# Hybrid decoder layer: the first half of x turned by plain products with the identity, the first weights loaded ahead of x's second tile, and linear attention's outputs by chunks in quarters of the array

## The chip, the cores and the metric

One core of a Trainium2 chip. The metric is device microseconds of one execution, median over runs; less is better. Before the change three runs gave 434.2, 435.39 and 435.99 us, median 435.39.

## What is computed

One decoder layer on 256 tokens of width 1024, in fp32. Cut to what the change touches:

```python
n    = rmsnorm(h, attn_norm)
proj = n @ w_in            # columns: g_q|g_k (512), g_v (512), g_r, g_al, d_q, d_k, d_v, gate_a, gate_b
# gated linear attention, chunks of 64 tokens, 4 heads, DK 64, DV 128
att     = einsum('bhncd,bhnsd->bhncs', q_dec, k_inv);  att = where(causal, att, 0)
o_intra = einsum('bhncs,bhnsv->bhncv', att, vc)
o_inter = einsum('bhncd,bhndv->bhncv', q_dec, s_prev)
o = o_intra + o_inter
...                        # differential attention, branch products, w_out, residual
h = h + hierarchical_moe(rmsnorm(h))     # 32 experts, top 2
h = h + sigmoid(h @ w_ple_gate) * rmsnorm(p @ w_ple);  out = rmsnorm(h, final_norm)
```

## The kernel before, in words

Tokens are two tiles `t` of 128. The first stage (to about 194 us) is a list of 114 *units*, most of them as follows: a unit is one 128x512 piece of a weight matrix (256 KB). `raw_load` (L342) issues its load on SP's queue; `part` (L350) splits it into a high half (ScalarE copy, tile `..._h`) and a low half (VectorE subtract, tile `..._l`), because every product is done as three fp32r products (`mm3`, L416: high x high, high times low of x, low times high of x). The unit then runs six products of 512 columns, three for each token tile. `run` (L388) is the loop that orders everything by hand: it loads eight units ahead, splits three units ahead (`part(i + a)` for `a < 3`, then `part(i + 3)` after the unit's products), and every engine keeps program order (`Ordered`, L50, and L58, the one line under which all instructions stand).

x comes as four quarters of 128x512: token tile `t`, column half `n` (`load_x`, L121). TensorE turns it: `x_transposed(q)` (L298) makes eight transposes into two PSUM banks `pxT0q`, `pxT1q`; `x_parts(k)` (L304) copies block `k` of the turned x out of the banks into `xT` as a high half (ScalarE, with the gain `g_attn`) and a low half (VectorE). The first eight units (`gqk_0` to `gqk_7`, L454) are the eight blocks of x against the columns for g_q and g_k; `part(i)` for `i < 8` also makes `x_parts(i)`. Before the first unit TensorE runs two dummy products (`warm`, L138) on a tile of ones that VectorE fills (L136), and one small transpose `pv` (L294) for `g_attn`.

Linear attention (`gla_steps`, L541) runs between units. Its last part (L593 to 613), for each `t`: the bank `po` takes, for four heads, the masked scores `attT` (128x128, off-diagonal 64x64 blocks zero) times the values, and then for each 64-token chunk `c` two products of the decayed queries with the state. fp32 operands (not fp32r) go through TensorE as two passes: two records in the trace for one product.

After the first stage come the router and the experts: eight groups of four experts, whose weights are loaded into a ring of slots (`refill`, L217), a slot being free when the products on it are done.

Of the kernel before, what the change touches and what calls it, by code (L numbers as in the profile page):

```python
# [20 lines left out]
P = 128  # L21
T = 256
NT = T // P
D = 1024
KC = D // P
# [38 lines left out]
def kernel(  # L64
# [33 lines left out]
    def bank(name):  # L98
        return psb.tile([P, 512], F32, tag="pb", name=name)

    V, A, E, Y, Q = (Ordered(tc, e) for e in (nc.vector, nc.scalar, nc.tensor, nc.sync, nc.gpsimd))
# [6 lines left out]
    xn = slot(NSLOT - 1, [NT, D], F32, "xn")  # L108
    tmp = slot(9, [2048], F32, "tmp")
    early = slot(6, [2048], F32, "early")  # L110
# [10 lines left out]
    def load_x(t, n):  # L121
        Y.dma_start(xn[:, t, n * 512:(n + 1) * 512], xs[t * P:(t + 1) * P, n * 512:(n + 1) * 512])

    load_x(0, 0)
    Y.dma_start(av, attn_norm[0].rearrange("(k p) -> k p", p=P))
    load_x(1, 0)
    Q.dma_start(posi, positions[0].rearrange("(t p) -> t p", p=P))
    wr = cst.tile([P, KC, 40], F32, name="wr")
    brt = cst.tile([P, 40], F32, name="brt")


    warm = cst.tile([P, 1], F32, name="warm")
    V.memset(warm, 0.0)
    A.activation(warm, warm, AF.Sin)

    V.memset(early[:, 0:512], 1.0)  # L136
    pw = bank("warm")
    for _ in range(2):  # L138
        E.matmul(pw[:, 0:432], early[:, 0:P], early[:, 0:432], start=True, stop=True)
    ident = cst.tile([P, P], F32, name="ident")  # L140
    make_identity(nc, ident)
    halfpi = cst.tile([P, 1], F32, name="halfpi")
# [152 lines left out]
    V.tensor_copy(g_attn, pv[:, 0:8])  # L295
    xps = {}

    def x_transposed(q):  # L298
        for t in range(NT):
            xps[q, t] = bank(f"pxT{t}{q}")  # L300
            for j in range(4):
                E.transpose(xps[q, t][:, j * P:(j + 1) * P], xn[:, t, (4 * q + j) * P:(4 * q + j + 1) * P], ident)

    def x_parts(k, ts=range(NT)):  # L304
        q, j = k // 4, k % 4
        if (q, 0) not in xps:
            x_transposed(q)
        for t in ts:
            split(xT[0][:, k, t * P:(t + 1) * P], xT[1][:, k, t * P:(t + 1) * P], xps[q, t][:, j * P:(j + 1) * P], g_attn[:, k:k + 1])

# [31 lines left out]
    def raw_load(i):  # L342
        if i < len(units) and i not in raws and i not in parts and i >= state["i"]:
            src, kc, n, name = units[i][0]

            raws[i] = wst.tile([P, kc, n], F32, tag="w_raw", name=f"{name}_r", bufs=4) if (i + 2) // 4 % 2 else \
                more[:, (i + 2) % 4, :].rearrange("p (k n) -> p k n", k=kc)
            Y.dma_start(raws[i], src.rearrange("(k p) n -> p k n", p=P))

    def part(i):  # L350
        if i < len(units) and i not in parts:
            src, kc, n, name = units[i][0]
            if i == 0:
                x_parts(0, [0])
            elif i < KC:
                x_parts(i)
            if units[i][3]:
                tag, bufs = ("w_raw",) * 2 if i == state.get("last") else ("w_h", "w_l"), 4 if i == state.get("last") else None
                parts[i] = [wst.tile([P, kc, n], F32R, tag=tag[c], name=f"{name}_{'hl'[c]}", bufs=bufs) for c in range(2)]
                split(parts[i][0], parts[i][1], raws.pop(i), None)  # L360
            else:
                parts[i] = raws.pop(i)
            if i == 0:
                x_parts(0, [1])

    def step(n=1, lane=0):

# [20 lines left out]
    def run(upto):  # L388
        while state["i"] < upto:
            i = state["i"]  # L390
            for a in range(8):
                raw_load(i + a)
                if a < 3:
                    part(i + a)
            units[i][1](parts.pop(i))
            state["i"] = i + 1
            part(i + 3)
            raw_load(i + 8)
            if units[i][2]:
                units[i][2]()  # L400
            for lane in range(2):
                waits[lane] -= 1
                if waits[lane] <= 0:
                    waits[lane] = 2
                    step(lane=lane)
            if KC <= i < state.get("quiet", i + 1) and i % EVERY == EVERY - 1:
                if fill and not halves:
                    fill.pop()
                    refill(whole=False)
                if halves:  # L410
                    Y.dma_start(*halves.pop(0))

    state = {"i": 0}
    waits = [2, 2]

    def mm3(acc, a, b, first, last):  # L416

        E.matmul(acc, a[0], b[0], start=first, stop=False)
        E.matmul(acc, a[1], b[0], start=False, stop=False)
        E.matmul(acc, a[0], b[1], start=False, stop=last)  # L420

    def stream(aT, nk, w, c0, name, done, mk=acc_bank):

        acc = []

        def emit(k):
            def f(ws):
                if k == 0:
                    acc.extend(mk(f"{name}_{t}") for t in range(NT))
                for t in range(NT):  # L430
                    mm3(acc[t], [a[:, k, t * P:(t + 1) * P] for a in aT], [w_[:, 0, :] for w_ in ws], k == 0, k == nk - 1)
            return f

        for k in range(nk):
            units.append(((w[k * P:(k + 1) * P, c0:c0 + 512], 1, 512, f"{name}_{k}"), emit(k),
                          (lambda: done(acc)) if k == nk - 1 else None, True))
# [10 lines left out]
    gqk, gv = [gq[:, t, :] for t in range(NT)], [gq[:, 2 + t, :] for t in range(NT)]  # L447
# [4 lines left out]
    ke = glc[:, 1792:2048]  # L452
    gqk_acc = []
    stream(xT, KC, w_in, C_GQK, "gqk", gqk_acc.extend)  # L454
    for i in range(2):
        raw_load(i)
    for t in range(NT):
        load_x(t, 1)

# [75 lines left out]
    states = [None]  # L535
    Q.memset(gla[:, 0:1536], 0.0)
    Q.memset(glb[:, 0:2], 0.0)
    attT, qdT = [glb[:, t] for t in range(NT)], []
    ssa = cst.tile([P, NT, 4], F32, name="ssa")

    def gla_steps():  # L541
# [51 lines left out]
        for t in range(NT):  # L593
            po = bank(f"po{t}")
            cs = [c for c in range(2) if states[2 * t + c] is not None]

            def intra(h, c=None):
                r = slice(0, P) if c is None else slice(64 * c, 64 * c + 64)
                E.matmul(po[r, h * P:(h + 1) * P], attT[t][:, h, r], gv[t][:, h * P:(h + 1) * P], start=h == 0,
                                 stop=h == 3 and c not in cs)  # L600

            for h in range(3):
                intra(h)
            for c in range(2):
                intra(3, c)
            for c in cs:
                for hp in range(2):
                    E.matmul(po[64 * c:64 * c + 64, hp * 256:(hp + 1) * 256], qdT[t][:, 0, hp, 64 * c:64 * c + 64],
                                     states[2 * t + c][:, hp].rearrange("p j v -> p (j v)"), start=False, stop=hp == 1)
            for h in range(4):  # L610
                A.activation(scr, po[:, h * P:(h + 1) * P], AF.Square, accum_out=ssa[:, t, h:h + 1])
            V.tensor_copy(oa[t].rearrange("p h v -> p (h v)"), po)
            yield 1
# [816 lines left out]
```

## Time and profile before

| | before |
|---|---|
| runs (us) | 434.2, 435.39, 435.99; median 435.39 |
| profiled execution: time, span | 436.0 us, 434.4 us |
| TensorE busy | 401.2 us, 92% of the span |
| VectorE, ScalarE, GpSimd busy | 219.5, 155.4, 37.1 us |
| DMA | 139.18 MB, mean 320 GB/s |
| chain that ended last | TensorE 56%, DMA 39%, VectorE 2% |

The span runs from the first to the last instruction; the execution's own time is 1.6 us longer. The chain that ended last is read back from the last instruction: the share of an engine in it is time that the end waited for that engine. In the timeline a record of TensorE lasts from its start to its modelled end, longer than the distance to the next record's start, since products overlap; distances between starts say what one costs.

### The profile page before, as it was taken

The page shows a single profiled execution, that of the slowest core. Times are in us where ns is not written, and L with a number is a line of the kernel's source. Part 1 is how long each engine was busy: PE and PEld are TensorE (multiplying, and loading weights), DVE is VectorE, ACT ScalarE, POOL GpSimd, SP SyncE. Part 2 cuts the span into 40 slices and gives each one's busy share as a digit, 9 for nine tenths or more (in the row PEclk, how much of TensorE's full clock was granted, in tenths as well). Part 3 has the DMA queues.
Part 4 walks back from the last instruction along what each step waited for, and adds up shares of the span by engine and source line. Part 5 has one row for each costly group of instructions (what it writes and reads, how often), then busy time and mean ns, then how long its engine had stood idle before and what let it go on. Part 6 is the DMA issues. An engine that isn't in the chain of part 4 may idle for free.

```text
span 434.4 us, 7552 instructions
## 1 busy us (share of the span) xinstructions
PE 401.2 (92%) x2876; PEld 275.6 (63%) x2876; DVE 219.5 (51%) x477; ACT 155.4 (36%) x335; POOL 37.1 (9%) x84
## 2 busy tenths in 40 slices
PE   8999999999999999999898988898798999889990
PEld 5777777778888888888454545455255266446770
DVE  4765764797889578667303221222131143535455
ACT  5747645488756645545000000000010100043344
POOL 7220005000080000001000000000000000000004
PEclk9999999999999999999999999999999799999996
DMA  7879974778898988896699999999999999999902
GB/s 258 232 219 322 310 246 148 240 231 297 274 274 297 306 303 283 272 345 280 241 425 417 422 411 419 416 422 420 421 418 420 422 420 418 401 364 368 331 6 97
DMA packets 47070, 139.18 MB, mean 320 GB/s; under 512 B 7266, under 2 KB 17206, under 8 KB 37816
## 3 DMA queue, kind: packets, MB, share of 16 engines
q1 hardware_dynamic: 46728, 138.35, 86.2%
q8 instruction: 23, 0.38, 0.4%
q10 hardware_dynamic: 144, 0.26, 0.2%
q14 instruction: 15, 0.12, 0.1%
q0 software_dynamic: 160, 0.07, 0.1%
HBM read 137.62 MB, written 1.05 MB: 319 GB/s over the span
## 4 chain that ended last, share of the span: by engine, by line
PE 56%; DMA 39%; DVE 2%; issue 1%; ACT 1%; POOL 0%; SPq 0%; POOLq 0%; DVEq 0%
DMA wt<-in_w_down_dram 14%; DMA wt<-in_w_up_dram 14%; PE sg L58 10%; DMA wt<-in_w_gate_dram 9%; PE y L58 6%; PE pg L58 5%; PE wo L58 5%; PE ph L58 3%; PE gqk L58 3%; PE dv L58 3%; PE dk L58 3%; PE gr L58 3%; PE pyq L58 2%; PE pxg L58 2%; DMA dq_r<-in_w_in_dram 1%; PE dq L58 1%
## 5 line engine op out<-in xcount | busy, mean ns | idle before, releaser
L58 PE MATMUL ph<-wt,xg 128*32 128x256 f32 x1024 | 62.5, 380 | 1.8 <-DMA wt<-in_w_up_dram 1.8
L58 PEld LDWEIGHTS ph<-wt,xg 128*32 128x32 f32 x1024 | 35.7, 110 | 24.8 <-DMA wt<-in_w_up_dram 3.1
L58 ACT ACTIVATE misc<-ph 128x256 f32<-128x256 f32 x8 | 3.1, 383 | 114.0 <-PE ph L58 114.0
L58 PE MATMUL sg<-sg_h,xT 128*128 128x512 f32 x128 | 40.4, 396 | 0.0
L58 PE MATMUL py<-wt,misc 128*32 128x512 f32 x192 | 30.9, 656 | 7.4 <-DVE misc L58 4.7
L58 PEld LDWEIGHTS pxg<-pq,xh 128*128 128x128 f32 x256 | 29.7, 192 | 4.9 <-issue 2.3
L58 PE MATMUL pxg<-pq,xh 128*128 128x128 f32 x256 | 30.5, 277 | 1.9 <-PEq L1067 1.6
L58 PE MATMUL pg<-wg,h2T 128*128 128x512 f32 x96 | 25.8, 404 | 0.7 <-ACT h2T L58 0.7
L58 PEld LDWEIGHTS sg<-sg_h,xT 128*128 128x128 f32 x128 | 23.4, 188 | 4.4
L58 PE MATMUL sg<-sg_l,xT 128*128 128x512 f32 x64 | 25.1, 392 | 0.0
L58 PEld LDWEIGHTS py<-wt,misc 128*32 128x32 f32 x192 | 6.8, 116 | 26.2 <-issue 13.7
L58 DVE SCALAR_TENSOR_TENSOR misc<-df,wr 128x128 f32<-128x128 bf16 x16 | 4.0, 288 | 37.7 <-PE phT L58 37.7
L58 POOL TENSOR_TENSOR sgs<-hn,rows 128x512 f32<-128x512 f32 x3 | 3.8, 1275 | 223.4 <-DVE hn L58 223.3
L58 DVE TENSOR_TENSOR xg<-pxg,g_exp 128x512 f32<-128x512 f32 x16 | 11.0, 690 | 23.2 <-PE pxg L58 22.9
L58 PEld LDWEIGHTS pg<-wg,h2T 128*128 128x128 f32 x96 | 16.6, 188 | 6.4 <-issue 2.5
L58 PE MATMUL wo<-wo_h,mT 128*128 128x512 f32 x64 | 20.0, 394 | 0.0
L58 PE MATMUL y<-y_h,oT 128*128 128x512 f32 x64 | 19.9, 392 | 0.0
L58 PE MATMUL y<-late,misc 128*128 128x512 f32 x32 | 14.9, 609 | 0.0
L58 DVE TENSOR_TENSOR sg_l<-sg_r,sg_h 128x512 fp32r<-128x512 f32 x16 | 12.6, 791 | 3.7 <-ACT sg_h L58 3.1
L58 PEld LDWEIGHTS sg<-sg_l,xT 128*128 128x128 f32 x64 | 12.0, 188 | 2.8 <-DVE sg_l L58 0.2
L58 DVE TENSOR_TENSOR sg_l<-more_r,sg_h 128x512 fp32r<-128x512 f32 x16 | 11.7, 743 | 3.9 <-ACT sg_h L58 2.8
L58 PEld LDWEIGHTS y<-y_h,oT 128*128 128x128 f32 x64 | 11.9, 188 | 2.3
(329 smaller groups left out, 757.5 us busy)
## 6 DMA issues: line engine op xcount, KB each, us to landing
wt<-in_w_up_dram SPq DMA_DIRECT2D x28, 1024.0 KB, 19.8
wt<-in_w_gate_dram SPq DMA_DIRECT2D x24, 1024.0 KB, 19.8
wt<-in_w_down_dram SPq DMA_DIRECT2D x20, 1024.0 KB, 20.0
wt<-in_w_down_dram SPq DMA_DIRECT2D x24, 512.0 KB, 9.3
more_r<-in_w_in_dram SPq DMA_DIRECT2D x42, 256.0 KB, 4.0
wt<-in_w_gate_dram SPq DMA_DIRECT2D x16, 512.0 KB, 5.7
wt<-in_w_up_dram SPq DMA_DIRECT2D x8, 512.0 KB, 4.4
sg_r<-in_w_in_dram SPq DMA_DIRECT2D x16, 256.0 KB, 3.0
```

The source lines that it names most:

```text
L58: ins = getattr(self.engine, name)(*args, **kwargs)
```

## The change

1. The dummy products read one column of ones, broadcast, so that VectorE fills 128x1 and not 128x512; they are 496, 496 and 64 columns, not twice 432.
2. `load_x(1, 0)` (second tile, first half) is issued after the first unit's weights, not before.
3. The first half of x (`q == 0`) is turned by ordinary products with the identity as the moving operand, not by transposes.
4. The second tile's turning and its copies are emitted between the first unit's products for tile 0 and those for tile 1; the weights of unit 0 are split ahead of x's copies; only unit 0 is split before it runs.
5. `po`: the four heads' products on `attT` go by 64x64 diagonal blocks (8 products of 64 rows and 64 columns for each `t`, not 3 of 128x128 and 2 of 128x64), and the products with the state alternate between the chunks.

```diff
     load_x(0, 0)
     Y.dma_start(av, attn_norm[0].rearrange("(k p) -> k p", p=P))
-    load_x(1, 0)
...
+    one = early[:, 0:1]
+    V.memset(one, 1.0)
     V.memset(warm, 0.0)
+    pw = bank("warm")
+    for n in (496, 496, 64):
+        E.matmul(pw[:, 0:n], one.to_broadcast([P, P]), one.to_broadcast([P, n]), start=True, stop=True)
     A.activation(warm, warm, AF.Sin)
-
-    V.memset(early[:, 0:512], 1.0)
-    pw = bank("warm")
-    for _ in range(2):
-        E.matmul(pw[:, 0:432], early[:, 0:P], early[:, 0:432], start=True, stop=True)
...
-    def x_transposed(q):
-        for t in range(NT):
+    def x_transposed(q, ts=range(NT)):
+        for t in ts:
             xps[q, t] = bank(f"pxT{t}{q}")
             for j in range(4):
-                E.transpose(xps[q, t][:, j * P:(j + 1) * P], xn[:, t, (4 * q + j) * P:(4 * q + j + 1) * P], ident)
+                src, dst = xn[:, t, (4 * q + j) * P:(4 * q + j + 1) * P], xps[q, t][:, j * P:(j + 1) * P]
+                if q == 0:
+                    E.matmul(dst, src, ident, start=True, stop=True)
+                else:
+                    E.transpose(dst, src, ident)
...
-        if (q, 0) not in xps:
-            x_transposed(q)
+        x_transposed(q, [t for t in ts if (q, t) not in xps])
...
-            if i == 0:
-                x_parts(0, [0])
-            elif i < KC:
+            if 0 < i < KC:
                 x_parts(i)
...
             if i == 0:
-                x_parts(0, [1])
+                x_parts(0, [0])
...
-                if a < 3:
+                if a < (3 if i else 1):
                     part(i + a)
...
                 for t in range(NT):
+                    if state["i"] == 0 and t == 1:
+                        x_parts(0, [1])
                     mm3(acc[t], ...)
...
-    for i in range(2):
-        raw_load(i)
+    raw_load(0)
+    load_x(1, 0)
+    raw_load(1)
...
-            def intra(h, c=None):
-                r = slice(0, P) if c is None else slice(64 * c, 64 * c + 64)
-                E.matmul(po[r, h * P:(h + 1) * P], attT[t][:, h, r], gv[t][:, h * P:(h + 1) * P], start=h == 0,
-                                 stop=h == 3 and c not in cs)
-
-            for h in range(3):
-                intra(h)
-            for c in range(2):
-                intra(3, c)
-            for c in cs:
-                for hp in range(2):
-                    E.matmul(po[64 * c:64 * c + 64, hp * 256:(hp + 1) * 256], qdT[t][:, 0, hp, 64 * c:64 * c + 64],
-                                     states[2 * t + c][:, hp].rearrange("p j v -> p (j v)"), start=False, stop=hp == 1)
+            rc = [slice(64 * c, 64 * c + 64) for c in range(2)]
+            for h in range(4):
+                for c in range(2):
+                    E.matmul(po[rc[c], h * P:(h + 1) * P], attT[t][rc[c], h, rc[c]], gv[t][rc[c], h * P:(h + 1) * P],
+                             start=h == 0, stop=h == 3 and c not in cs)
+            for hp in range(2):
+                for c in cs:
+                    E.matmul(po[rc[c], hp * 256:(hp + 1) * 256], qdT[t][:, 0, hp, rc[c]],
+                             states[2 * t + c][:, hp].rearrange("p j v -> p (j v)"), start=False, stop=hp == 1)
```

What this makes of the order on the engines, at three places. First ScalarE, from its first copy on, before (`gqk_1_h` is the high half of unit 1's weights, `pxT00` and `pxT10` the banks of the turned x of tiles 0 and 1, `xT0` its high halves):

```order
L58 ACTIVATE xT0_128<-pxT00_160,early_73 128x128 [waits DVE_49,PE_49]
L58 ACTIVATE gqk_0_h_172<-more_r_137 128x512 [waits DMAHW3_49]
L58 ACTIVATE xT0_128<-pxT10_165,early_73 128x128 [waits PE_49]
L58 ACTIVATE xT0_128<-pxT00_160,early_73 128x128 [waits DVE_49]
L58 ACTIVATE xT0_128<-pxT10_165,early_73 128x128 [waits DVE_49]
L58 ACTIVATE gqk_1_h_182<-more_r_137 128x512 [waits DMAHW4_49]
L58 ACTIVATE xT0_128<-pxT00_160,early_73 128x128 [waits DVE_49]
L58 ACTIVATE xT0_128<-pxT10_165,early_73 128x128 [waits DVE_49]
L58 ACTIVATE gqk_2_h_192<-gqk_2_r_186 128x512 [waits DMAHW7_49]
```

and of the change:

```order
L58 ACTIVATE gqk_0_h_161<-more_r_137 128x512 [waits DMAHW2_49]
L58 ACTIVATE xT0_128<-pxT00_165,early_73 128x128 [waits DVE_49,PE_49]
L58 ACTIVATE xT0_128<-pxT10_187,early_73 128x128 [waits PE_49]
L58 ACTIVATE xT0_128<-pxT00_165,early_73 128x128 [waits DVE_49]
L58 ACTIVATE xT0_128<-pxT10_187,early_73 128x128 [waits DVE_49]
L58 ACTIVATE gqk_3_h_201<-gqk_3_r_174 128x512 [waits DMAHW0_49]
L58 ACTIVATE xT0_128<-pxT00_165,early_73 128x128 [waits DVE_49]
L58 ACTIVATE xT0_128<-pxT10_187,early_73 128x128 [waits DVE_49]
L58 ACTIVATE gqk_1_h_210<-more_r_137 128x512 [waits DMAHW4_49]
L58 ACTIVATE xT0_128<-pxT00_165,early_73 128x128 [waits DVE_49]
L58 ACTIVATE xT0_128<-pxT10_187,early_73 128x128 [waits DVE_49]
L58 ACTIVATE gqk_2_h_218<-gqk_2_r_172 128x512 [waits DMAHW7_49,PE_49,Activation_49]
```

Unit 0's weights have moved ahead of x's copies, and unit 3's weights with unit 3's two copies of x ahead of those of units 1 and 2: in `run`, unit 0 now runs with only itself split, and the next statement is `part(0 + 3)`. On VectorE the low halves follow in the same order.

TensorE at the start, of the change (`gqk_0_182` and `gqk_1_183` are the banks of tiles 0 and 1):

```order
L58 MATMUL warm_82<-early_73 128x496 x2
L58 MATMUL warm_82<-early_73 128x64
L58 MATMUL pv_132<-ident_87,tmp_72 128x8
L58 MATMUL pxT00_165<-ident_87,xn_71 128x128 x4
L58 MATMUL gqk_0_182<-gqk_0_h_161,xT0_128 128x512
L58 MATMUL gqk_0_182<-gqk_0_h_161,xT1_129 128x512
L58 MATMUL gqk_0_182<-gqk_0_l_162,xT0_128 128x512
L58 MATMUL pxT10_187<-ident_87,xn_71 128x128 x4
L58 MATMUL gqk_1_183<-gqk_0_h_161,xT0_128 128x512
L58 MATMUL gqk_1_183<-gqk_0_h_161,xT1_129 128x512
L58 MATMUL gqk_1_183<-gqk_0_l_162,xT0_128 128x512
L58 MATMUL gqk_0_182<-gqk_1_h_210,xT0_128 128x512
```

Tile 1's turning stood before the first product of unit 0, and stands now in the middle of the unit.

TensorE at the outputs of linear attention, of the change (`glb` holds `attT` and the turned queries, `gla` the states, `gq` the values):

```order
L58 MATMUL po0_815<-gq_138,glb_150 64x128 [waits PE_49]
L58 MATMUL po0_815<-gq_138,glb_150 64x128 x7
L58 MATMUL po0_815<-gla_149,glb_150 64x256 x2
L58 MATMUL dv_0_831<-dv_0_h_763,xT0_128 128x512 [waits Activation_49]
L58 MATMUL dv_0_831<-dv_0_h_763,xT1_129 128x512
```

Eight products of 64x128 stand where three of 128x128 and two of 64x128 stood; what is before and behind them is unmoved.

## Rows read from the trace of the kernel before

**Rows 1.** The chain that ended last, in order of time: start us, us, what, and how many pieces were merged.

```profile
7.15 4.81 PE gqk L58 x12
...
193.23 0.50 PE wo L58 x3
...
205.87 7.04 PE ph L58 x128
...
232.10 13.34 DMA wt<-in_w_down_dram
...
360.03 19.60 DMA wt<-in_w_up_dram
```

**Rows 2.** Busy time of each engine in three stretches (from:to us, length, then busy us and instructions of each engine, granted clock, DMA share, GB/s).

```profile
202.00:210.00 8.00, 8.00 (x114) 6.10 (x116) 4.94 (x19) 2.70 (x11) 0.00 (x0) 1.00 0.13 54
210.00:380.00 170.00, 152.27 (x1458) 82.27 (x1452) 44.93 (x109) 9.01 (x21) 0.00 (x0) 0.97 1.01 416
7.15:193.70 186.55, 185.91 (x938) 148.97 (x939) 136.22 (x276) 115.35 (x252) 25.69 (x43) 1.00 0.83 273
```

**Rows 3.** TensorE's timeline at the start: start us, us, engine, line, operation, out<-in, array shape, tile, count of merged records.

```profile
1.68 3.25 PE L58 MATMUL warm<-early 128*128 128x432 f32 x4 [1.68 <-DVE early L58]
4.86 0.27 PE L58 MATMUL pv<-ident,tmp 8*128 8x8 f32 x1
5.06 1.97 PE L58 MATMUL pxT<-ident,xn 128*128 128x128 f32 x8
7.15 1.22 PE L58 MATMUL gqk<-gqk_h,xT 128*128 128x512 f32 x2
8.16 0.63 PE L58 MATMUL gqk<-gqk_l,xT 128*128 128x512 f32 x1
8.59 1.05 PE L58 MATMUL gqk<-gqk_h,xT 128*128 128x512 f32 x2
...
11.79 1.04 PE L58 MATMUL pxT<-ident,xn 128*128 128x128 f32 x8
12.58 0.70 PE L58 MATMUL gqk<-gqk_h,xT 128*128 128x512 f32 x2
...
14.05 0.62 PE L58 MATMUL gqk<-gqk_h,xT 128*128 128x512 f32 x2
```

**Rows 4.** ScalarE's timeline from its first copy of the turned x (same columns; in brackets the idle time before and what ended it).

```profile
6.21 0.37 ACT L58 ACTIVATE xT<-pxT,early 128x128 fp32r<-128x128 f32 x1 [3.79 <-PE pxT L58]
6.47 0.62 ACT L58 ACTIVATE gqk_h<-more_r 128x512 fp32r<-128x512 f32 x1
7.06 0.62 ACT L58 ACTIVATE xT<-pxT,early 128x128 fp32r<-128x128 f32 x2
8.11 0.37 ACT L58 ACTIVATE xT<-pxT,early 128x128 fp32r<-128x128 f32 x1 [0.43 <-DVE xT L58]
8.38 0.62 ACT L58 ACTIVATE gqk_h<-more_r 128x512 fp32r<-128x512 f32 x1
8.90 0.61 ACT L58 ACTIVATE xT<-pxT,early 128x128 fp32r<-128x128 f32 x2
```

**Rows 5.** VectorE's timeline, its first two instructions and the low halves of the first units.

```profile
1.00 0.06 DVE L58 MEMSET warm<- 128x1 f32 x1 [1.00 <-PEq L1416]
1.14 0.48 DVE L58 MEMSET early<- 128x512 f32 x1
...
7.13 0.69 DVE L58 TENSOR_TENSOR gqk_l<-more_r,gqk_h 128x512 fp32r<-128x512 f32 x1 [0.17 <-ACT gqk_h L58]
7.74 0.60 DVE L58 SCALAR_TENSOR_TENSOR xT<-pxT,early,xT 128x128 fp32r<-128x128 f32 x2
```

**Rows 6.** SP's queue at the start, its issues (start us, us, out<-in, count), and under them the loads by tile over the first 20 us and for the issue at 1.79 alone (count, KB each, median us from issue to landing).

```profile
1.79 0.36 SPq L58 DMA_DIRECT2D xn<-in_x_dram  x1
...
4.08 2.09 SPq L58 DMA_DIRECT2D gqk_r<-in_w_in_dram  x4
...
gqk_r<-in_w_in_dram SPq DMA_DIRECT2D x4, 256.0 KB, 5.4
...
xn<-in_x_dram SPq DMA_DIRECT2D x1, 256.0 KB, 3.8
```

**Rows 7.** TensorE's timeline at linear attention's products: the scores `pa`, the state updates `pu` (16 records of two chunks, then 8 of one), the outputs `po` of tile 0 and what follows them (the pair `64*64` is the part of the array that a product takes, rows by columns).

```profile
47.15 0.71 PE L58 MATMUL pa<-glb 64*128 64x128 f32 x8
...
49.39 0.68 PE L58 MATMUL pu<-gq,glc 64*64 64x128 f32 x16
...
62.13 0.40 PE L58 MATMUL dk<-dk_l,xT 128*128 128x512 f32 x1
62.46 0.65 PE L58 MATMUL pu<-gq,glc 64*64 64x128 f32 x8
...
65.90 1.20 PE L58 MATMUL po<-gq,glb 128*128 128x128 f32 x10
66.94 1.03 PE L58 MATMUL po<-gla,glb 128*64 128x256 f32 x4
67.89 0.72 PE L58 MATMUL dv<-dv_h,xT 128*128 128x512 f32 x2
```

## The prediction

> **What bounds the kernel now.** I read the chain of waits first, then the busy time by stretches, then the timelines of the two places that change. The chain [rows 1] starts on TensorE with unit 0's products at 7.15, stays in the unit stage until the last `wo` product at 193.23, goes through the first experts (`ph` at 205.87), and is in the experts' weight loads from 232.10 to the load that starts at 360.03. The stretches [rows 2] say the same: TensorE is busy 185.91 of the 186.55 us from 7.15 to 193.70. Between 210 and 380 the DMA share is 1.01 at 416 GB/s: there the loads are the bound. But from 202 to 210 that share is 0.13: the ring of slots is full, and the loads go on when `ph` frees slots. So the loads' stage begins when the experts' first products run, and those when the unit stage ends. A microsecond won or lost before 193 us therefore reaches the end, as long as TensorE really is the one that waits.
>
> **The first microseconds, before.** TensorE's timeline [rows 3]: dummy products from 1.68, `pv` at 4.86, eight transposes from 5.06 (1.97 us), unit 0 at 7.15. The clock shows in the products' distances. Two fp32r products with 1.05 us end to end, one being 0.63, are 0.42 apart at 8.59; at 14.05 it is 0.62 less 0.39, 0.23. That is the step between the two levels, 1.2 and 2.4 GHz: TensorE runs at the lower one until about 11 us, though it was busy almost all the time from 1.68. The chain has 4.81 us for the twelve products of units 0 and 1 [rows 1]; at 0.23 they would be 2.76. About 2.05 us lie there to be won. After eight more transposes unit 2 starts at 12.58 [rows 3], and from then on nothing differs between the kernels until `po`. So **unit 2's start is where I compare**: 12.58 before.
>
> **The start after, step by step.** Dummy products: VectorE's 128x1 fill takes the 0.06 us of the row at 1.00 where 0.48 us were taken from 1.14 [rows 5], so TensorE starts about 0.55 us earlier, at 1.12. But 2x(496+496+64) columns at the lower clock, scaled from 3.25 us for 2x864 [rows 3], are 3.9 to 4.0 us, and `pv` comes at 5.1, not 4.86. Nothing won; the cover is that x's data and the identity are needed then anyway.
>
> Loads: the first weights take the second place in the queue. What stood there, x's second tile, was issued at 1.79 and landed 3.8 us later [rows 6], at 5.6. ScalarE's high half of unit 0 then runs 5.65 to 6.25, VectorE's low half to 6.95 (0.62 and 0.69 us, [rows 4, 5]). That is off the path, before x arrives.
>
> Turning tile 0: four products with fp32 operands are eight passes, where four transposes were four records. The transposes cost 0.21 us each at the lower clock, 0.11 at the higher (1.97 and 1.04 us for eight, less the last one's tail, [rows 3]). A pass of an fp32 product of 128 columns also costs 0.10 at the higher clock (`po`: 1.20 us for ten, [rows 7]). From 5.3 the eight passes end at 6.4 with the higher clock, at 7.3 with the lower.
>
> With the higher clock: x's copy (0.37) ends 6.8, its low half (0.35) waits for VectorE and ends 7.3. TensorE's three products for tile 0 start at 6.8, 7.3 and 7.5. Now tile 1's eight passes follow, 7.75 to 8.75; before, they were over before unit 0 began. Copies again (0.37 + 0.35): products at 9.2, 9.55, 9.8, **unit 0 over at 10.0**. Before, unit 0 was over at 9.87 (three products from 8.59 at 0.43, [rows 3]). The clock's gain is used up by two more passes for each block and by the copies that TensorE now waits for twice.
>
> Then the order: ScalarE has unit 3's two copies and unit 3's weights ahead of unit 1's. Unit 3's load is the second of the four from 4.08 (some 0.5 apart), lands 5.4 us after its issue [rows 6], at 9.95. ScalarE's queue stands at 9.85 by then, so it goes on at 10.0. It takes 0.53 for unit 3's weights, twice 0.26 for unit 1's copies, and 0.62 for unit 1's weights (distances in [rows 4]): 11.7. VectorE behind it: unit 3's low half 10.65 to 11.25, unit 1's two low x halves to 11.8, unit 1's low weights to 12.5 (0.61 and 0.26 apart, [rows 5]). TensorE idles from 10.0 to 11.7, does two products, waits until 12.5, does four more: 13.4. The eight transposes of x's second half take 0.8: **unit 2 at 14.2, 1.6 us later than before**. Unit 2's own split is done by 13.7, so nothing more is added.
>
> How early the clock rises no row shows; I bound it. If it comes only with the end of tile 0's passes, the copies start 0.9 later and, through the wait for unit 3's load, unit 2 starts at 14.8 (+2.2). If only at 11.0 as before, tile 1's passes end near 10.9 and unit 2 starts at 16.2 (+3.6). If the data and the copies overlap better than I have them, unit 1 need not wait for unit 3's split: +0.1. I take +1.6, the early rise, since TensorE then has had nothing but products from 1.12.
>
> SP's queue: unit 1's release of its buffer comes 2.5 us later, and with it the loads behind it in that queue; those are for units that run 8 us later, so nothing waits.
>
> **The outputs of linear attention.** Before, ten passes of `po` hold TensorE from 65.90 to 66.94, 1.04 us [rows 7]. After, 16 passes on 64x64 quarters. The nearest row is `pu`, eight passes on quarters of one row half, 0.054 us apart (0.65 less a tail of 0.27, over seven); pairs overlap. So do pairs of `pa`, in row halves. At 0.054 the 16 take 0.86. Entering another array shape costs about 0.1: from `dk` at 62.13 to `pu` is 0.33, where 0.23 is usual. The new order has two such entries ahead of the states' products, the old one. Net -0.18 + 0.1, and as much for the pairs' slower first step: 0 to +0.1, I take **+0.1 for each tile, +0.2**. Low end: four quarters at once, `pu` x16 at 0.027, -0.4 each. High end: 16 passes one after the other at 0.107 with the entries, 1.9 us, +0.9 each.
>
> **Sum.** +1.6 + 0.2 = +1.8 on the profiled 436.0; the median of the runs, 435.39, lies 0.6 below it, which makes 437.2. One thing speaks for less: the profiled rise at 11 us came soon after the products began, and in an execution where it comes later, before loses 0.5 us for each us of it. I take 0.4 off: **436.8 us**, its own range 435.8 to 437.9 (+0.4 to +2.5). A measurement of this kernel tells about 0.5% from no change, 2.2 us.
>
> **Rivals.**
> *The clock pays.* If the split of unit 3 does not hold unit 1 up, and the copies of x hide, the twelve products cost 2.05 less: 435.39 - 2.05 = 433.3. For it: that time is in the chain. Against it: ScalarE's order, which is fixed, and the landing at 9.95. Chance 0.15. The Trainium skill (TensorE: Matmul & The Clock Gate, Part 4: PE-mode transpose) says that transposes do not count as busy for the clock, so products in their place would bring the rise forward. The trace agrees so far as it stayed low through the transposes to 7.0; by that rule the rise comes early, which the sum has already.
> *The quarters do not overlap* (slower). Both diagonal quarters write one bank, `po`, from different row halves. No row shows that: `pa` pairs row halves in two banks, `pu` pairs column halves in one. It decides if the passes of a pair start over 0.1 us apart; then +0.9 twice instead of +0.1 twice: 436.8 + 1.6 = 438.4. Chance 0.15. The Trainium skill (TensorEngine Tiling (Array Packing), Gotcha 1: PSUM Pressure) says that different row tiles cannot access the same bank at once, which is this case. By that rule it would be 438.4; I hold the overlap in `pu` for nearer, as partitions differ.
> *The clock rises as late as before* (slower): 435.4 + 3.6 + 0.2 = 439.2, if the columns and gaps of the new start are no more to it than those of the old. Chance 0.1.
> *Nothing reaches the end*, because the unit stage has slack that the chain does not show: 435.4. Chance 0.05; 0.64 us of idle in 186 speaks against it.
>
> **How the numbers follow.** My case has 0.55: about three tenths of it lie above 437.6. Slower by over 0.5%: 0.55 x 0.3 = 0.165, nearly all of the two slower rivals, 0.12 and 0.09: 0.37. Faster by over 0.5% (under 433.2): half of the first rival, 0.08. Within: 0.55. The range takes in the first rival's 433.3 and most of the late clock: 433.3 to 439.2.
>
> **What would show it.** Right: unit 0's first product near 6.8, its tile 1 near 9.2, a gap on TensorE before unit 1 of 1 to 2 us ended by ScalarE, unit 3's high half on ScalarE ahead of unit 1's, unit 2 near 14.2; distances of 0.23 from unit 0 on; `po` pairs within 0.01 us, about 1.1 us for 16 passes. Wrong: no gap before unit 1, unit 2 before 12.6, or `po` passes 0.1 apart.

## The result, and the profile after

The change is slower: median 440.47 us (440.14 to 441.24, 4 runs) against 434.92 us (434.2 to 435.99, 4 runs), 5.55 us between the medians. The ratio on record is 1.0116 with a 95% interval of 1.009 to 1.0141, so about 5.0 us (3.9 to 6.1); here and below a difference in time is worked out from the ratio on record, which is not the quotient of the medians. The prediction had 436.8 and a range to 439.2. The profiled execution took 441.24 us, its span is 439.6 us, 5.2 longer than before's 434.4, and the sum below is made on the spans.

TensorE's timeline at the start, after (columns as in [rows 3]):

```profile
1.11 3.99 PE L58 MATMUL warm<-early 128*128 128x496 f32 x6 [1.11 <-DVE warm L58]
5.04 0.27 PE L58 MATMUL pv<-ident,tmp 8*128 8x8 f32 x1
5.24 1.49 PE L58 MATMUL pxT<-ident,xn 128*128 128x128 f32 x8
7.18 0.89 PE L58 MATMUL gqk<-gqk_h,xT 128*128 128x512 f32 x2 [0.46 <-ACT xT L58]
7.91 0.39 PE L58 MATMUL gqk<-gqk_l,xT 128*128 128x512 f32 x1
8.13 1.05 PE L58 MATMUL pxT<-ident,xn 128*128 128x128 f32 x8
9.64 0.89 PE L58 MATMUL gqk<-gqk_h,xT 128*128 128x512 f32 x2 [0.46 <-ACT xT L58]
10.37 0.40 PE L58 MATMUL gqk<-gqk_l,xT 128*128 128x512 f32 x1
12.25 0.79 PE L58 MATMUL gqk<-gqk_h,xT 128*128 128x512 f32 x2 [1.49 <-ACT gqk_h L58]
13.06 0.79 PE L58 MATMUL gqk<-gqk_l,xT 128*128 128x512 f32 x1
13.65 1.05 PE L58 MATMUL gqk<-gqk_h,xT 128*128 128x512 f32 x2
14.50 0.63 PE L58 MATMUL gqk<-gqk_l,xT 128*128 128x512 f32 x1
14.93 1.66 PE L58 MATMUL pxT<-ident,xn 128*128 128x128 f32 x8
16.34 0.72 PE L58 MATMUL gqk<-gqk_h,xT 128*128 128x512 f32 x2
```

Read it from below. Unit 2 starts at 16.34; before it was 12.58 [rows 3]. Unit 1 starts at 12.25, behind 1.49 us of idle that ScalarE ended; before it started at 9.87, behind no gap at all:

```profile
9.87 1.05 PE L58 MATMUL gqk<-gqk_h,xT 128*128 128x512 f32 x2
```

From 13.65 on, a pair of products lasts 1.05 and a single one 0.63, as at the lower clock before 11 us in [rows 3]; ahead of the gap, at 7.91 and 10.37, the single one lasted 0.39 to 0.40. So the clock was up, and fell again. The stretches show it (columns as in [rows 2]; the granted clock is the third number from the right):

```profile
12.80:16.20 3.40, 3.38 (x11) 2.65 (x11) 1.32 (x4) 0.70 (x3) 0.00 (x0) 0.50 0.69 203
16.20:20.00 3.80, 3.80 (x19) 3.15 (x19) 3.16 (x9) 3.55 (x11) 0.00 (x0) 1.00 0.28 91
215.00:385.00 170.00, 152.25 (x1460) 82.24 (x1454) 44.91 (x109) 9.02 (x21) 0.00 (x0) 0.97 1.01 415
```

In the trace's clock records the granted clock goes up at 5.95, down at 12.78 and up at 16.19: the lower level, 1.2 GHz, for most of the stretch from unit 1 to unit 2. Ahead of the fall TensorE had no work from 10.76 to 12.25, and before that two gaps of 0.46, which end at 7.18 and 9.64. The last row is the loads' stage, taken 5 us later than in [rows 2] and the same but for 1 GB/s. The first product of the experts (`ph`) starts at 211.10, before at 205.80, 5.3 later, and the span is longer by nearly the same: the delay was carried there one for one.

ScalarE, after (answers to [rows 4]), shows what the gap waits for:

```profile
5.83 0.63 ACT L58 ACTIVATE gqk_h<-more_r 128x512 fp32r<-128x512 f32 x1 [3.41 <-DMA more_r<-in_w_in_dram]
...
9.22 0.62 ACT L58 ACTIVATE xT<-pxT,early 128x128 fp32r<-128x128 f32 x2 [2.09 <-PE pxT L58]
10.01 0.37 ACT L58 ACTIVATE xT<-pxT,early 128x128 fp32r<-128x128 f32 x1 [0.16 <-DVE xT L58]
10.53 0.63 ACT L58 ACTIVATE gqk_h<-gqk_r 128x512 fp32r<-128x512 f32 x1 [0.16 <-DMA gqk_r<-in_w_in_dram]
11.07 0.61 ACT L58 ACTIVATE xT<-pxT,early 128x128 fp32r<-128x128 f32 x2
11.57 0.63 ACT L58 ACTIVATE gqk_h<-more_r 128x512 fp32r<-128x512 f32 x1
```

Unit 3's weights (`gqk_r`, in at 10.5) are split at 10.53, unit 1's (`more_r`, issued at 2.66, where unit 3's were at 4.56) only at 11.57. Unit 1 cannot begin before that. Two things hold ScalarE up here, one behind the other: it stands 2.09 us until 9.22 for the turning of tile 1, and then it has unit 3's work ahead of unit 1's. For unit 3's load itself it waits only 0.16 us.

Linear attention's outputs, tile 0 (answers to [rows 7]):

```profile
70.40 1.09 PE L58 MATMUL po<-gq,glb 64*64 64x128 f32 x16
71.42 1.08 PE L58 MATMUL po<-gla,glb 128*64 128x256 f32 x4
72.43 0.73 PE L58 MATMUL dv<-dv_h,xT 128*128 128x512 f32 x2
```

From `po` to `dv` 2.03 us, before 1.99. The trace's single records of a pair start 0.007 us apart, the pairs 0.102: the quarters overlap. With the entry, from the last product ahead of `po` to the first behind it, tile 0 takes 2.35 us (before 2.22) and tile 1 2.36 (before 2.27): both together cost 0.22.

Last, a wait that the prediction did not have. VectorE and TensorE at the router, after:

```profile
202.23 0.16 DVE L58 SCALAR_TENSOR_TENSOR sinT<-ss 128x1 f32<-128x1 f32 x1 [0.78 <-ACT wo L58]
203.43 0.26 DVE L58 SCALAR_TENSOR_TENSOR lg<-pr,sinT,brt 128x40 f32<-128x40 f32 x1 [1.04 <-PE pr L58]
```

```profile
202.82 0.51 PE L58 MATMUL pr<-wr,h1T 128*128 128x40 f32 x3
203.16 1.36 PE L58 MATMUL idle<-ident 128*128 128x128 f32 x10
205.79 0.18 PE L58 MATMUL pk<-Mb,scr 128*128 128x32 bf16 x1 [1.27 <-DVE r_g L58]
```

and before:

```profile
197.97 0.26 DVE L58 SCALAR_TENSOR_TENSOR lg<-pr,sinT,brt 128x40 f32<-128x40 f32 x1 [0.16 <-PE pr L58]
```

```profile
200.48 0.18 PE L58 MATMUL pk<-Mb,scr 128*128 128x32 bf16 x1 [0.54 <-DVE r_g L58]
```

The first `lg`, which reads tile 0's router products, now waits until tile 1's are over as well. From the start of the last `pr` to `pk` it is 2.75 us (203.04 to 205.79), before 2.01 (198.47 to 200.48): 0.74 more.

So the 5.2 us are: unit 1 later by 2.38, from unit 1 to unit 2 another 1.38 (4.09, not 2.71), `po` 0.22, router 0.74, and 0.62 between unit `gv` and the last `dk` product ahead of `po` (43.10, before 42.48), less about 0.1 elsewhere. In that stretch VectorE waits for a small load until 45.02 (before 40.61), and TensorE then stands:

```profile
46.28 0.50 PE L58 MATMUL dq<-dq_l,xT 128*128 128x512 f32 x1 [0.96 <-DVE dq_l L58]
```

That wait is not tied to the change: from `gv` to `po` it is 43.42 after and 42.71 before, in the runs below between 41.89 and 43.91, and 43.36 in run 8, which has only the new dummy products.

### The profile page after: what moved, and what is told of

Its sections match the earlier page's. It is cut to its first block, busy times and chain, and to the rows that moved or that the text cites. A ratio compares the mean times of both kernels' runs of the same rounds, so it can differ in the third digit from the quotient of the medians.

```text
span 439.6 us, 7592 instructions
## 1 busy us (share of the span) xinstructions
PE 403.2 (92%) x2898; PEld 276.2 (63%) x2898; DVE 218.5 (50%) x477; ACT 155.7 (35%) x335; POOL 37.2 (8%) x84
## 3 DMA queue, kind: packets, MB, share of 16 engines
HBM read 137.62 MB, written 1.05 MB: 315 GB/s over the span
## 5 line engine op out<-in xcount | busy, mean ns | idle before, releaser
L58 PE MATMUL gqk<-gqk_h,xT 128*128 128x512 f32 x32 | 11.3, 431 | 2.4 <-ACT gqk_h L58 1.5
```

The lines of the kernel that those rows point to most:

```text
L58: ins = getattr(self.engine, name)(*args, **kwargs)
```

## The experiments

**Theory A**: the order of the splits (0, 3, 1, 2) makes the gap, the gap lets the clock fall, and the router's wait belongs to it too. **Theory B**: the rest of the start (twice as many passes, tile 1 turned in the middle of unit 0, the loads' order) costs the time. **Theory C**: a delay at the start costs more at the end than its own length. Numbers behind a label: median (runs), ratio to the kernel before on the same chip with its 95% interval. The medians are from several chips, where the kernel before had 436.83 (runs 1 to 4), 436.28 (5 to 8) and 435.69 (9 to 12), so compare by the ratio. "u1", "u2" are the starts of units 1 and 2, "router" is from the start of the last `pr` to `pk` (the expectations call it "end of pr to pk"), "rise" the time at which the granted clock goes up, all of the profiled execution.

| run | us | ratio | u1 | u2 | router | rise |
|---|---|---|---|---|---|---|
| before | 434.92 (4) | 1 | 9.87 | 12.58 | 2.01 | 11.01 |
| the change | 440.47 (4) | 1.0116, 1.009 to 1.0141 | 12.25 | 16.34 | 2.75 | 5.95, falls 12.78 |
| 1 change, splits in order | 438.19 (12) | 1.0046, 1.0025 to 1.0068 | 11.49 | 14.04 | 2.01 | 5.81 |
| 2 change, gap filled | 439.65 (6) | 1.0083, 1.0052 to 1.0114 | 13.11 | 15.75 | 2.75 | 6.92 |
| 3 before, unit 2 delayed | 440.14 (6) | 1.0102, 1.0067 to 1.0136 | 9.19 | 15.56 | 2.02 | 7.03 |
| 4 before + quarters | 436.61 (12) | 1.0004, 0.9976 to 1.0032 | 9.18 | 11.73 | 2.02 | 5.26 |
| 5 before + order of splits | 439.77 (12) | 1.0091, 1.0057 to 1.0124 | 12.10 | 14.72 | 2.75 | 10.79 |
| 6 run 1, transposes | 438.58 (12) | 1.0046, 1.0011 to 1.0081 | 10.43 | 12.99 | 2.01 | 6.02 |
| 7 run 1, tile 1 first | 436.62 (12) | 1.0011, 0.9983 to 1.0038 | 9.46 | 12.01 | 2.02 | 5.83 |
| 8 before + dummies | 435.79 (12) | 0.9992, 0.9959 to 1.0024 | 9.27 | 11.83 | 2.02 | 6.20 |
| 9 change, `lg` moved | 440.02 (8) | 1.0088, 1.0059 to 1.0118 | 12.40 | 16.39 | 1.63 | 5.90, falls 12.72 |
| 10 run 7, transposes | 437.57 (12) | 1.0046, 1.0017 to 1.0075 | 10.43 | 12.72 | 2.02 | 10.66 |
| 11 before + products | 436.92 (12) | 1.0014, 0.9987 to 1.0042 | 9.96 | 12.50 | 2.02 | 4.72 |
| 12 before + loads' order | 436.29 (12) | 0.9991, 0.9959 to 1.0023 | 9.87 | 12.48 | 2.01 | 10.80 |

**1. The change with the splits in order.**

```diff
-            part(i + 3)
+            for b_ in range(1, 4):
+                part(i + b_)
```

> The change, but after unit 0 the splits are made in the order of units 1, 2, 3, not 3, 1, 2; all else is the change's. Theory A (the order on ScalarE makes the gap before unit 1, the gap lets the clock fall, and the other order also gives the router's first scores another wait): the gap before unit 1 shrinks from 1.5 us to under 0.7, TensorE stays at the higher clock from unit 0 on, unit 2 starts near 13.0 (the change 16.34, before 12.58), the 0.7 us at the router goes, and the time is 1.0 us or less above before. Rival B (turning tile 1 in the middle of unit 0 by twice as many passes is what costs): unit 2 stays near 15 to 16 and the time 3 us or more above before.

The fall of the clock is gone, from unit 1 to unit 2 it is 2.55 us (after: 4.09), unit 2 starts 2.30 earlier, and the router has its 2.01 again. So far A. But the time is 2.0 us above before, twice what A allowed, and unit 2 comes at 14.04, not 13.0: unit 0's second tile begins only at 10.19 and unit 1 at 11.49.

```profile
10.19 0.89 PE L58 MATMUL gqk<-gqk_h,xT 128*128 128x512 f32 x2 [0.46 <-ACT xT L58]
11.49 0.73 PE L58 MATMUL gqk<-gqk_h,xT 128*128 128x512 f32 x2 [0.18 <-ACT gqk_h L58]
```

(TensorE's timeline of this run.) Something of B is there too.

**2. The change with the gap filled** by two dummy products behind unit 0.

```diff
             units[i][1](parts.pop(i))
+            if i == 0:
+                for n in (496, 400):
+                    E.matmul(pw[:, 0:n], one.to_broadcast([P, P]), one.to_broadcast([P, n]), start=True, stop=True)
```

> The change, with two dummy products of 496 and 400 columns on TensorE between unit 0 and unit 1, where it stood idle for 1.5 us; the order of the splits stays 3, 1, 2. Theory A: unit 1 still starts near 12.3, but the clock does not fall at 12.8, units 1 and the eight transposes run at 0.23 and 0.11, unit 2 starts near 14.7 instead of 16.34, and the time is 1.6 us below the change's. Rival (the clock falls for another reason, or the gap's length is what matters): the clock still falls near 13, unit 2 at 16 or later, no gain.

```profile
11.06 1.67 PE L58 MATMUL warm<-early 128*128 128x496 f32 x4
13.11 0.73 PE L58 MATMUL gqk<-gqk_h,xT 128*128 128x512 f32 x2 [0.38 <-ACT gqk_h L58]
```

(TensorE's timeline of this run.) With TensorE busy in the gap the clock stays up until 218 us, and unit 1 to unit 2 takes 2.64: the fall costs 1.45 us, and the idle time is what it follows. Unit 2 gained only 0.59, since unit 1 itself began 0.86 later in this execution (13.11; 12.3 was expected); the ratio's interval overlaps that of the change. The mechanism is shown, its gain in time is not.

**3. The kernel before, with unit 2 delayed** by 3.76 us of dummy products behind unit 1.

```diff
             units[i][1](parts.pop(i))
+            if i == 1:
+                for n in (432, 432, 432, 432, 432, 96):
+                    E.matmul(pw[:, 0:n], early[:, 0:P], early[:, 0:n], start=True, stop=True)
```

> The kernel before, with 3.76 us of dummy products on TensorE between unit 1 and unit 2, at the higher clock: a late start of unit 2 by what the change has, and nothing else of it. If a delay reaches the end one for one: unit 2 at 16.3, and +3.8 us at the end. Theory C (a later unit stage also makes DMA waits of its own: the lambda load that VectorE waits for near 41 lands still later): +0.8 more near 46, +4.6 at the end. If the unit stage has slack: less than +3.8. The router's first scores should start as in before, with no 0.7 us more, as this build has before's waits there.

Unit 2 is 2.98 us later than in before's profile and the experts' first `ph` 2.71; the time is 4.5 us longer (2.9 to 5.9), which holds the 3.83 to run 4's unit 2 at 11.73. The delay arrives at the end about one for one. The time alone would also hold C's 4.6; but the wait that C needs is not in this profile: `gv` to `po` is 42.49, before 42.71. Nothing here speaks for C, and a small part of it is not ruled out.

**4. The kernel before with linear attention's quarters alone.** The change's last part of the diff on `po`, nothing else.

> The kernel before with the outputs of linear attention by quarters alone. The quarters cost +0.05 to +0.1 us for each tile. This build has, like the change, the longer wait of the router's first scores on VectorE: Theory A's third part says +0.7 us at the router, so +0.8 to +0.9 us at the end in all. If that wait is an accident of one execution: +0.1 to +0.2.

No difference that can be measured, and `po` to `dv` is 2.03 us as in the change. The expected 0.7 at the router did not come: a miss. That wait is not tied to the quarters.

**5. The kernel before with the order of the splits alone.**

```diff
-                if a < 3:
+                if a < (3 if i else 1):
```

> The kernel before with one statement of the change: only unit 0 is split before it runs, so that the splits come in the order 0, 3, 1, 2. Theory A (the order of the splits is the largest part of the loss): unit 3's weights land near 10.0 to 10.5, ScalarE does them ahead of unit 1's, unit 1 starts near 11.5 to 12.2 after a gap on TensorE of 1.5 us or more (no gap in the kernel before), and unit 2 at 14.2 if the clock stays high, near 16 if it falls back as it did in the changed kernel; the router's wait (end of pr to pk) is 2.75, not 2.01. Together 2.5 to 4.5 us above the kernel before. Theory B (the order hurts only because tile 1 is turned in the middle of unit 0): unit 2 at 12.6 to 13.2 and the time within 0.8 us of the kernel before.

```profile
9.79 0.63 PE L58 MATMUL gqk<-gqk_l,xT 128*128 128x512 f32 x1
12.10 0.73 PE L58 MATMUL gqk<-gqk_h,xT 128*128 128x512 f32 x2 [1.68 <-ACT gqk_h L58]
```

That is TensorE's timeline of this run; on ScalarE's stands:

```profile
10.38 0.63 ACT L58 ACTIVATE gqk_h<-gqk_r 128x512 fp32r<-128x512 f32 x1 [1.55 <-DMA gqk_r<-in_w_in_dram]
```

One condition makes 4.0 us of the loss (2.5 to 5.4): the gap before unit 1, 1.68 us here, and the router's 2.75. A is right, and its alternative, that the order hurts only with tile 1 in mid-unit, falls. Here ScalarE does stand 1.55 us for unit 3's load. In the change tile 1's turning held it up over the same time, so the two losses cover each other: unit 1 starts at 12.10 with this order alone, at 11.49 with the turning in mid-unit and the splits in order (run 1), and at 12.25 with both. The clock rose only at 10.79 in this execution, inside the gap (10.42 to 12.10), and did not fall behind it.

**6. Run 1 with transposes in place of products.**

```diff
-                if q == 0:
+                if q < 0:
```

> The changed kernel with the splits in order 1, 2, 3 (as in the first experiment) and the first half of x turned by transposes again, not by products. Theory B1 (twice as many records on TensorE cost what they look like): about 0.4 us less for each tile at the high clock, unit 2 at 13.2 against 14.04, and the time 0.5 to 0.9 us below the first experiment's +2.0, that is 1.1 to 1.5 above the kernel before. Theory B2 (the products are what brings the clock up early): the clock rises at 7 to 11 us and unit 2 comes at 14 to 16, the time the same as or above the first experiment. Theory B3 (the passes hide behind the waits for loads and copies): the same as the first experiment within 0.3 us.

Unit 2 at 12.99 is 1.05 earlier than in run 1, as B1 has it, and the clock rose early without products, at 6.02. The time decides nothing: the same ratio, with an interval that holds B1's 1.1 to 1.5 us as well as B3.

**7. Run 1 with tile 1 turned and copied ahead of unit 0.**

```diff
             if i == 0:
                 x_parts(0, [0])
+                x_parts(0, [1])
...
-                    if state["i"] == 0 and t == 1:
-                        x_parts(0, [1])
```

> The changed kernel with the splits in order 1, 2, 3, products, and the second tile turned and copied ahead of unit 0's first product, no longer in its middle. Theory B4 (the turning in mid-unit makes TensorE wait for copies twice): no gap inside unit 0, its tile 1 starts 1.0 us after its first product (10.19 less 7.37 = 2.8 in the first experiment), unit 1 near 10.3, unit 2 near 12.9: about 1.1 us below the first experiment, 0.9 above the kernel before. Rival (the time goes to the loads, and tile 1's x was late anyway): unit 0's first product moves back by as much, to 8.2 or later, and unit 2 stays at 13.7 to 14.1.

```profile
7.45 0.70 PE L58 MATMUL gqk<-gqk_h,xT 128*128 128x512 f32 x2
7.99 0.40 PE L58 MATMUL gqk<-gqk_l,xT 128*128 128x512 f32 x1
8.23 0.81 PE L58 MATMUL gqk<-gqk_h,xT 128*128 128x512 f32 x2
8.88 0.40 PE L58 MATMUL gqk<-gqk_l,xT 128*128 128x512 f32 x1
9.46 0.73 PE L58 MATMUL gqk<-gqk_h,xT 128*128 128x512 f32 x2 [0.18 <-ACT gqk_h L58]
```

(TensorE's timeline of this run.) The gap inside unit 0 is gone: tile 1 starts 0.78 behind tile 0 (run 1: 2.82), though unit 0 begins only 0.08 later. Unit 2 is at 12.01, 2.03 earlier than in run 1, more than expected. With splits in order and tile 1 first, everything else of the change is still in this kernel, and its time cannot be told from before's. Against the change the intervals do not touch: the two placements together hold nearly the whole loss, 1.0116 less 1.0011, some 4.6 us.

**8. The kernel before with the new dummy products alone** (the change's first item).

> The kernel before with the new dummy products alone (496, 496 and 64 columns from one broadcast column, starting about 0.5 us earlier). If longer and earlier dummies make the early rise of the clock more frequent, unit 2 starts at 11.7 in the profile (12.58 in that of the kernel before, 11.73 in the run with linear attention's quarters alone) and the time is 0.4 to 0.9 us below the kernel before. If the early rise comes as often without them: the same within 0.3 us.

No difference that can be measured. The rise came at 6.20; in runs 3 and 4, with the old dummies, at 7.03 and 5.26.

**9. The change, with the router's small tiles placed elsewhere**: `onesb`, `lg`, `Mb`, `rk` and the `r_` tiles are taken from their pool ahead of `misc`.

```diff
+    onesb = wk.tile([P, P], BF16, name="onesb")
+    lg = wk.tile([P, NT, 40], F32, name="lg")
...
     misc = wk.tile([P, D], F32, name="misc")
...
-    onesb = wk.tile([P, P], BF16, name="onesb")
...
-    lg = wk.tile([P, NT, 40], F32, name="lg")
```

> The changed kernel whole, but the router's small tiles (lg and those behind it) are taken first from their pool, so that they no longer lie where the last half of the turned tokens lay, which TensorE's last router products still read. Theory (the router's 0.73 us is a wait for memory, placed elsewhere by the order of the splits): the first lg starts right behind the first tile's products as in the kernel before, end of pr to pk 2.0 us, not 2.75; the time 0.7 us below the changed kernel's, ratio to the kernel before 1.008 to 1.010. Rival (the wait is for the products themselves): 2.75 stays. The start is untouched, so it also shows a second time what the clock does there: if the fall after the gap belongs to this order, unit 2 starts near 16.3 again; if it was of that one execution, near 14.9.

```profile
202.88 0.26 DVE L58 SCALAR_TENSOR_TENSOR lg<-pr,sinT,brt 128x40 f32<-128x40 f32 x1
```

```profile
12.40 0.97 PE L58 MATMUL gqk<-gqk_h,xT 128*128 128x512 f32 x2 [1.22 <-ACT gqk_h L58]
13.21 0.80 PE L58 MATMUL gqk<-gqk_l,xT 128*128 128x512 f32 x1
13.81 1.05 PE L58 MATMUL gqk<-gqk_h,xT 128*128 128x512 f32 x2
14.66 0.63 PE L58 MATMUL gqk<-gqk_l,xT 128*128 128x512 f32 x1
```

(VectorE at the router, and TensorE at units 0 to 1.) `lg` has no idle time before it and `pk` comes 1.63 behind the last `pr`: the wait was for memory, which the last `pr` still read. The pool `wk` lies on the space of the first stage's buffers; in the kernels whose splits run 0, 3, 1, 2 (the change, runs 2 and 5) `lg` waits so, in the other ten it does not. The addresses that the kernels give their tiles show the link. `lg` lies at byte 221248 of each partition in all kernels but this one (217152). The 2048 bytes from 220992 on belong to `h1T11`, the tile that the last four products of the router read, in the change and runs 2, 5 and 9, and to `h1T10`, which is read before it, in the other ten: the order of the splits swaps the two. The second thing this run shows: the clock falls at 12.72, behind a gap of 1.22 us, and unit 2 starts at 16.39. The fall came in both profiles of this start, so it is not of one execution. The gain in time, 1.0088 against 1.0116, is inside the intervals.

**10. Run 7 with transposes.**

> What is left of the change when its three losses are undone: new dummy products, unit 0's weights ahead of x's second tile, linear attention's quarters; splits in order 1, 2, 3, both tiles turned by transposes ahead of unit 0. Theory B1 (each half of the doubled passes costs 0.3 to 0.65 where nothing hides it, by the run with transposes): unit 0 at 6.7 to 7.0, unit 2 at 11.2 to 11.6 against 12.01 with products and 12.58 in the kernel before; the time 0.3 to 0.8 us below the kernel before. Rival (x's second tile, landing near 6.4 behind unit 0's weights, is now what unit 0 waits for): unit 0 at 7.4 or later, unit 2 at 11.8 to 12.2, the time the same as the kernel before within 0.3 us.

```profile
6.95 1.12 PE L58 MATMUL pxT<-ident,xn 128*128 128x128 f32 x4 [0.59 <-DMA xn<-in_x_dram]
7.72 1.20 PE L58 MATMUL gqk<-gqk_h,xT 128*128 128x512 f32 x2
```

(TensorE's timeline of this run.) Unit 0 is as the rival has it: x's second tile is waited for. But unit 2 (12.72) and the time missed both forecasts, and the clock rose only at 10.66. Why the time is 2.0 us above before's (0.7 to 3.3), when unit 2 starts at 12.72 and the profiled span is 434.8, stays open.

**11. The kernel before with products in place of transposes alone** (the change's third item), and **12. with the loads' order alone** (the second).

> The kernel before, with the first half of x turned by products with the identity in place of transposes and nothing else. In the five runs so far that turn it so, the clock rose between 5.8 and 6.9; in the seven with transposes it rose four times between 5.3 and 7.0 and three times between 10.7 and 11.0. Theory B2 (the products bring the early rise): it rises before 7 again, unit 0 starts at 7.4 to 7.6 (sixteen passes instead of eight records), unit 2 at 11.8 to 12.0, and the time is 0 to 0.6 us below the kernel before. Rival (the early rise is chance, and the passes cost 0.4 to 0.8): the time 0.2 to 0.8 us above the kernel before, and the rise may come near 11.

> The kernel before, with the first unit's weights issued ahead of x's second tile and nothing else. Theory (x's second tile, landing near 6.4 in place of 5.6 to 6.0, holds up its transposes): a gap of 0.3 to 0.6 us ended by the load of xn, as in the last run of the set before, unit 0 at 7.4 to 7.7, and the time 0.2 to 0.6 us above the kernel before. Rival (unit 0's weights, split earlier, win it back): unit 0 at 7.0 to 7.2 and the same time within 0.2 us.

Neither can be told from no change. In 11 the clock rose at 4.72 and stayed up, but unit 0 then waited 1.02 us for its weights' high half, and unit 2 came at 12.50:

```profile
8.05 0.74 PE L58 MATMUL gqk<-gqk_h,xT 128*128 128x512 f32 x2 [1.02 <-ACT gqk_h L58]
```

(TensorE's timeline of run 11.) In 12 the second tile's transposes did not wait: unit 0 at 7.14.

No run beat the kernel before: the lowest ratios, 0.9991 and 0.9992, have intervals that hold 1.

## Why the prediction was wrong

**Right: the place and the cause of the gap.** Unit 2's start was the place to compare, and a delay there reaches the end (run 3). ScalarE had unit 3's split ahead of unit 1's, came to it about when unit 3's load was in (forecast 9.85 and 9.95, measured 10.4 and 10.5), and did unit 1's behind it. The gap was forecast at 1 to 2 us and is 1.49; run 5 shows that this order alone makes most of the loss.

**The step that failed: "distances of 0.23 from unit 0 on".** The working had the clock rise early, which it did (5.95), and then held it up through a gap that the same working had put there. It fell at 12.78, half a microsecond behind the gap's end, and from unit 1 to unit 2 it took 4.09 where the prediction's 11.7 to 14.2 is 2.5: 1.59 of the 2.14 us by which unit 2 came later than forecast (16.34, not 14.2). In run 2 the fall is gone when the gap is filled; in run 9 it comes again. The rival with the late clock came near the time, 439.2, by luck: its mechanism, a rise as late as before's, did not happen.

**Mis-sized: unit 1's start.** 11.7 was forecast, 12.25 measured, 0.55 more: the first product at 7.18, not 6.8, tile 1 at 9.64, not 9.2, and unit 3's load in at 10.5, not 9.95.

**Not in the sum: the router's 0.74.** "... from then on nothing differs between the kernels until `po`", and nothing named behind it: that looked at the order of instructions alone. Where tiles lie, and so what they wait for, changed with the order of the splits (run 9).

**Right: `po`.** +0.2 was forecast for both tiles, 0.22 measured, and nothing that the time shows (run 4). The two quarters of a pair write one bank, `po`, from different row halves, start 0.007 us apart, and the 16 passes take 1.09 us, where the rival had 1.9 with the entries for passes one after the other. The Trainium skill (TensorEngine Tiling (Array Packing), Gotcha 1: PSUM Pressure) says that different row tiles cannot access the same bank at once. No cost of that kind is seen here.

**The clock at the start.** The prediction took 0.4 us off for executions in which before's clock rises later than in its profile. That term had the wrong sign: no profile with transposes shows a rise later than 11.01, and before's own start had an earlier one in runs 3 and 4, with unit 2 at 11.73 in the second, 0.85 earlier. In the six profiles that turn x by products the clock rose by 6.92 each time; in the eight with transposes four times by 7.03 and four times between 10.66 and 11.01. The Trainium skill (TensorE: Matmul & The Clock Gate, Part 4: PE-mode transpose) says that transposes do not count as busy in the same way. The four early rises show that transposes there don't prevent the rise; the dummy products ran ahead of it in all fourteen profiles, and fourteen do not settle whether more products make it surer. No gain in time was seen: run 11 is 1.0014 (0.9987 to 1.0042).

**Of theory B**, turning tile 1 in mid-unit is the real part in the profiles: run 1 against run 7, 2.03 us at unit 2. By the ratios it is 1.5, but their intervals overlap, so its share of the time is not shown by itself. The prediction said that the copies would be waited for twice, and that they and the doubled passes use up the early clock's gain; the two gaps of 0.46 and the end of unit 0, 10.76 where 10.0 was forecast, bear that out.

## What to carry to other kernels

When a change lets an engine run dry at the start, price the gap and then what the clock does behind it: here 1.49 us of idle cost about another 1.4. Before moving a statement in a loop that splits or loads ahead, list the order that each engine gets and ask whether the next unit's data now stands behind a later unit's load. A reordering far upstream can swap where two tiles lie and so put a wait at the other end of the program: look at the first users of every pool that reuses memory.

## What was not expected of the hardware

The granted clock fell to the lower level behind 1.22 to 1.49 us of idle on TensorE (12.72, 12.78) and was back at 16.14 and 16.19, while a gap of 1.68 us in which the clock rose, at 10.79, was followed by no fall (run 5), and neither was a gap of 1.02 us behind a rise at 4.72 (run 11). With the same start, before and run 4 differ in when the clock first rises by 5.75 us (11.01 and 5.26) and in unit 2's start by 0.85; part of the spread of the runs may come from there, which no run shows.
